# A hybrid attention layer on one core: streaming the first branch's value weights, and moving the forget gate and four modulation weights

## The chip, the cores and the metric

The kernel runs on one core of a Trainium2 chip. The metric is device time in microseconds (us). The engines are TensorE (matmuls; PE in the profile, with its weight loads as PEld), VectorE (DVE), ScalarE (ACT), GpSimd (POOL) and SyncE (SP, which here issues the loads). "Product" below means one matmul with 512 columns.

## The reference

One decoder layer for 512 tokens of width 1024, in float32. A modulation vector comes from a conditioning vector `c`. Two causal attention branches of 8 heads each run on the same modulated input:

```
mod = c @ w_ada + b_ada                        # six vectors: shift, scale, gate, twice
u = x * (1 + sc1) + sh1
q_a, k_a, v_a, f_a, q_b, k_b, v_b, g_a, g_b = split(u @ w_in)
# branch 0 (FoX): softmax(q k^T / 8 + cum_t - cum_s) v, cum = cumsum(log sigmoid(f_a + b_forget))
# branch 1 (stick-breaking): A[t,s] = beta[t,s] * prod_{s<j<t} (1 - beta[t,j]),  A v
merged = sigmoid(g_a) * (y_fox @ w_fox_proj) + sigmoid(g_b) * (y_sb @ w_sb_proj)
x = LN(alpha * x + (1 + gt1) * (merged @ w_o))
...                                            # gated MLP with a causal depthwise conv, second LN
```

## The kernel before

Every weight product is made of three matmuls: each operand is split into a high part (rounded to the matmul's format, `hi_of`, an ACT copy, line 75) and a low part (`lo_of`, a DVE subtraction, line 78), and high x high, high x low and low x high are summed. The modulated input stands as `uh[k]`, `ul[k]`, eight tiles of 128 channels by 512 tokens.

**Weights.** `items` is a list of weight blocks in the order of use, 128x1024 each. `weights(i)` lets SP load up to four items ahead into four raw buffers (tag `raw`), and lets ACT and DVE split up to two items ahead, by the item's own function: `split_proc` makes a high and a low 128x1024 tile, each from three rotating buffers (`wh`, `wl`). Items of the modulation matrix (`ada_proc`) lie among them. The first eight of the 24 in this part are accumulated on DVE (line 581), the others are summed on DVE with one instruction into a column (`mod_col`, lines 169 and 174).

**Filling products.** `stream` is a list of generators that issue products (`proj`, the values, `bproj`). The loop over the 16 heads (`heads`, first 8 of branch 1, then 8 of branch 0) works with three steps a head: `stage_a` (scores, line 473 and 474; then sigmoids and a scan on DVE, or softmax), `stage_b` (transposes, line 529), `stage_c` (weighted sum over the values, line 547). Between them `fill(n)` draws n products from `stream`, and `fill_to(mark)` draws until a mark. A mark is reached before the step that needs it: `v1` before the first `stage_c`, the pair's `k` before its `stage_a`. `lim` bounds how far the stream may be drawn; until n is 6 it is the mark `v0`, in front of branch 0's values.

The order on SP is that of the program. The order on the other engines comes from a planner that goes by its own cost model and takes the program's order as priority. PSUM has eight banks, which all steps share.

**Values.** For branch 1 (stick-breaking), `v_proc` splits the four value weights into sixteen 512-wide tiles (`wvh`, `wvl`) that stay, and `vproj` makes one block of 128 tokens after the other, 24 products each in one bank (lines 430 to 432). After each block `v_diff` copies the bank to SBUF (`vf`, line 392), moves it down by one row with transfers on POOL's queue (`dv`, lines 396 and 397), subtracts (line 399) and splits the difference (`v_evac`). For branch 0, `vgroup` already holds four banks open, one for each block, and streams the weights (lines 446 to 448); its `v_evac` calls follow all products.

**Forget gate.** `forget(after)` computes the log of the sigmoid on ACT (lines 323 to 325), its cumulated sum on DVE (line 327) and a split (`chi`), and `decay_rows` sends rows of it with POOL's queue (lines 341 and 342) to the operands of branch 0's scores. It is called at the start of n = 6.

**Order of the stream.** Pair 1 of q and k, branch 1's values, pair 2, pair 3 and two gates, branch 0's values with a modulation weight behind each group, pair 4, a gate, pairs 5, 6, 7 with one modulation weight behind each projection, then gates and projections of the outputs.

Of the kernel before, what the change touches and what calls it, by code (L numbers as in the profile page):

```python
# [9 lines left out]
F32R = mybir.dt.float32r  # L10
# [6 lines left out]
P = 128  # L17
T = 512
D = 1024
KT = D // P  # L20
NB = T // P
# [24 lines left out]
def layer_kernel(ctx: ExitStack, tc: tile.TileContext, out, xT, x, cT, crow, wa0, wa1, bcol, bgt, w1, wct, wv, bf,  # L46
# [3 lines left out]
    V, S, G, PE = nc.vector, nc.scalar, nc.gpsimd, nc.tensor  # L50
# [14 lines left out]
    def bank():  # L65
        return pp.tile([P, 512], F32, name=nm("ps"), tag="ps")
# [7 lines left out]
    def hi_of(o, i, scale=1.0):  # L74
        S.activation(o, i, AF.Copy, scale=scale)  # L75

    def lo_of(o, i, hi):
        return V.tensor_tensor(o, i, fl(hi), ALU.subtract)  # L78
# [32 lines left out]
    def z(dt, s, shape=(P, 512)):  # L111
        return zp.tile(list(shape), dt, name=nm(s), tag="z", bufs=NZ)
# [7 lines left out]
    items = []  # L120
    state = {"load": 0, "proc": 0}

    def add_item(src, proc, cols=1024):
        items.append([src, proc, cols, None, None])
        return len(items) - 1

    def weights(i, ahead=AHEAD):
        while state["load"] < min(len(items), i + LOADS):
            it = items[state["load"]]
            it[3] = stg.tile([P, 1024], F32, name=nm("raw"), tag="raw", bufs=LOADS)  # L130
            nc.sync.dma_start(it[3][:, 0 : it[2]], it[0])
            state["load"] += 1
            while state["proc"] <= state["load"] - LOADS:
                process()
        while state["proc"] < min(len(items), i + 1 + ahead):
            process()
        return items[i][4]
# [18 lines left out]
    uh, ul, w1s, mods = [], [], [], []  # L156
# [164 lines left out]
    def forget(after):  # L321
        with tc.issue_after(after.ins):
            S.activation(fq[0], fq[1], AF.Abs)
            S.activation(fq[0], fq[0], AF.Exp, scale=-1.0)
            S.activation(fq[0], fq[0], AF.Ln, bias=1.0)
        V.scalar_tensor_tensor(fq[1], fq[1], 0.0, fq[0], ALU.min, ALU.subtract)
        V.tensor_tensor_scan(fq[0], ones[0:NH, 0:1].broadcast_to([NH, 512]), fq[1], 0.0, ALU.mult, ALU.add)
        hi_of(chi[:, 0, :], fq[0])
        lo_of(chi[:, 1, :], fq[0], chi[:, 0, :])
        gated.append(True)  # L330
        for h in range(4):
            if idx(0, h) - 4 in scored:
                decay_rows(h)
# [56 lines left out]
    def v_diff(j, ps):  # L390
        vf, dv = z(F32, "vf"), z(F32, "dv")
        S.activation(vf, ps, AF.Copy)
        if j == 0:
            G.memset(dv[0:1, :], 0.0)
        else:
            G.dma_start(dv[0:1, :], vfs[-1][P - 1 : P, :])
        G.dma_start(dv[1:P, :], vf[0 : P - 1, :])
        vfs.append(vf)
        V.tensor_tensor(dv, vf, dv, ALU.subtract)
        for half in range(2):  # L400
            v_evac(1, j, half, dv)

    def v_evac(br, j, half, ps):
        vv = z(F32R, "vv")
        v3 = vv.rearrange("s (p q d) -> s p q d", q=4, d=64)
        p3 = ps[:, half * 256 : (half + 1) * 256].rearrange("s (p q d) -> s p q d", q=2, d=64)
        hi_of(v3[:, :, 0::3, :], p3)
        lo_of(v3[:, :, 1:3, :], p3, v3[:, :, 0::3, :])
        vt[(br, j, half)] = vv
# [2 lines left out]
        o = ((h // 2) % 2) * 256 + (h % 2) * P  # L412
        return vt[(br, j, h // 4)][:, o : o + P]

    def v_proc(r):
        t = []
        for e in range(2):
            h, l = z(F32R, "wvh"), z(F32R, "wvl")
            hi_of(h, r[:, e * 512 : (e + 1) * 512])
            lo_of(l, r[:, e * 512 : (e + 1) * 512], h)  # L420
            t.append((h, l))
        return t

    def vproj(br, j, last):
        ps = bank()
        weights(last)
        tb = slice(j * P, (j + 1) * P)
        for k in range(KT):
            h, l = items[wvi[k // 2]][4][k % 2]
            PE.matmul(ps, uh[k][:, tb], h, start=k == 0, stop=False)  # L430
            PE.matmul(ps, uh[k][:, tb], l, start=False, stop=False)
            PE.matmul(ps, ul[k][:, tb], h, start=False, stop=k == KT - 1)
            yield 3
        v_diff(j, ps)

    vbk = []

    def vgroup(q, n):
        if q == 0:
            vbk.extend(bank() for _ in range(NB))  # L440
        h, l = weights(n)
        for k in (2 * q, 2 * q + 1):
            c = slice((k % 2) * 512, (k % 2 + 1) * 512)
            for j in range(NB):
                tb = slice(j * P, (j + 1) * P)
                PE.matmul(vbk[j], uh[k][:, tb], h[:, c], start=k == 0, stop=False)
                PE.matmul(vbk[j], uh[k][:, tb], l[:, c], start=False, stop=False)
                PE.matmul(vbk[j], ul[k][:, tb], h[:, c], start=False, stop=k == KT - 1)
                yield 3
        if q == 3:  # L450
            for j in range(NB):
                for half in range(2):
                    v_evac(0, j, half, vbk[j])

    def proj(n, after):
        ps = bank()
# [148 lines left out]
    sg, ma, wps = {}, {}, {}  # L605
# [46 lines left out]
    stream, sums = [], []  # L652
# [4 lines left out]
    def add_ada(n=1):  # L657
        for _ in range(n):
            if skip[0]:
                skip[0] -= 1  # L660
            elif adas[0] < 24:
                add_item(wa1[adas[0]], ada_proc(adas[0]))
                adas[0] += 1
                if adas[0] in (4, 8):
                    stream.append((ada_split, (adas[0] // 4 - 1, len(items) - 1)))
                    sums.append([len(stream) + 1, adas[0] // 4 - 1])

    marks = {}
# [12 lines left out]
    def add_bproj(br, j, after):  # L681
        if j % 2 == 0:
            wpi[br] = add_item(wp[br, j // 2], split_proc)
        stream.append((bproj, (br, j, wpi[br], after)))

    def add_pair(p):
        br, pr = seq[p]
        for c, ev in (("q", q_evac), ("k", k_evac)):
            if (c, p) in TILES:
                add_proj((c, p), lambda ps, ev=ev: ev(br, pr, ps))  # L690
                marks[(p, c)] = len(stream)
                add_ada()

    wvi = []

    def add_gate(br, j):
        add_proj(("sb" if br == 1 else "fox", j), gate_after(br, j))
        add_ada()

    gb = list(range(NG, KT))  # L700
    for p, ng in ((1, 0), (2, 0), (3, 2), (4, 1)):
        if p == 4:
            marks["v0"] = len(stream)
            for j in range(4):
                stream.append((vgroup, (j, add_item(wv[0, j], split_proc))))
                add_ada()
        add_pair(p)
        if p == 1:
            for j in range(4):
                wvi.append(add_item(wv[1, j], v_proc))  # L710
            for j in range(NB):
                stream.append((vproj, (1, j, wvi[-1])))
            marks["v1"] = len(stream)
        for _ in range(ng):
            add_gate(1, gb.pop(0))
    add_pair(5)
    marks["y1"] = len(stream)
    bj = list(range(KT))
    for p in (6, 7):
        add_pair(p)  # L720
        for _ in range(4):
            if bj:
                j = bj.pop(0)
                add_bproj(1, j, lambda m, j=j: ma.__setitem__(j, m))

    mh, ml = [], []

# [37 lines left out]
    def fill(n):  # L765
        while n > 0:
            if cur["g"] is None:
                if cur["n"] >= lim[0]:
                    return
                f, a = stream[cur["n"]]  # L770
                cur["g"] = f(*a)
            try:
                n -= next(cur["g"])
            except StopIteration:
                cur["g"] = None
                cur["n"] += 1
# [19 lines left out]
    heads = [(br, 2 * p + e) for br, p in seq for e in range(2)]  # L796
    last = hd[heads[1]]['last']
    for n, (b, h) in enumerate(heads):
        if n == 6:
            forget(last)  # L800
        f1, f2, f3 = FILL[n // 8]
        if n + 2 < 16:
            if n == 6:
                lim[0] = marks["y1"]
            if n % 2 == 0:
                fill_to(marks[(n // 2 + 1, "k")])
            last = hd[heads[n + 1]].get("last")
            stage_a(*heads[n + 2])
        fill(f1)
        if n + 1 < 16:  # L810
            stage_b(*heads[n + 1])
        fill(f2)
        if n == 0:
            fill_to(marks["v1"])
            fill(15)
        stage_c(b, h)
        if n == 7:
            lim[0] = marks["y0"]
        if n == 15:
            lim[0] = len(stream)  # L820
        fill(f3)
# [133 lines left out]
    for n in range(2 * FT):  # L955
        if n < NSPLIT:
            h, l = items[wui[n]][4]
            ps = bks[n]
            up_mm(ps, h, l, slice(256, 512))
        else:  # L960
            ps = bank()
# [49 lines left out]
    for i in range(NB):  # L1011
        tb = slice(i * P, (i + 1) * P)
        r = x1[i]
# [96 lines left out]
```

## Time and profile before

| | |
|---|---|
| time of three runs | 776.55 us median, 775.83 to 776.66 |
| the profiled execution | 776.09 us, of which the span of instructions is 774.3 us |
| TensorE busy | 754.7 us in 3570 matmuls |
| VectorE busy | 541.6 us |
| ScalarE busy | 354.6 us |
| mean granted TensorE clock | 0.995 |

Times in the profile count from the start of the span. A busy row gives an engine's time in instructions; matmuls are pipelined, so their durations overlap (a product is recorded with some 0.39 us, and they follow each other at shorter distances). A row of waits reads: who waited <- for whom: us in total, times, longest. In a row of the timeline, the brackets at the end give the idle time in front of the instruction and what ended it.

### The profile page before, as it was taken

What the parts mean: (1) busy time and instruction counts of PE and PEld (TensorE: products, weight loads), DVE (VectorE), ACT (ScalarE), POOL (GpSimd) and SP (SyncE); (2) the same over time, 40 slices, a digit from 0 to 9 for tenths busy, and PEclk for the clock granted to TensorE, in tenths of its full rate; (3) what the DMA queues carried; (4) which work ended last, traced back from release to release, by engine and by line L of the source; (5) the groups of instructions that cost most, each with busy time, mean ns of one, the idle gap of its engine ahead of it and who ended that gap; (6) DMA issues with size and microseconds to landing.
All of it is one profiled execution on the core that took longest, in us unless ns stands there. A gap on an engine that the chain in (4) does not pass through costs nothing.

```text
span 774.3 us, 9546 instructions
## 1 busy us (share of the span) xinstructions
PE 754.7 (97%) x3570; PEld 622.2 (80%) x3570; DVE 541.6 (70%) x820; ACT 354.6 (46%) x592; POOL 146.2 (19%) x113
## 2 busy tenths in 40 slices
PE   8999989989999999999999999999999999999995
PEld 4878767868788888888889888888888888888885
DVE  6868748997778895476766887677656665534566
ACT  3568348854866555433145334444444433222300
POOL 1030100020100011353100680000000043945500
PEclk9999999999999999999999999999999999999998
DMA  8943621356331423444401614354332314332302
GB/s 330 404 151 135 218 82 55 117 180 221 110 114 51 137 84 131 139 165 154 149 1 55 218 58 160 110 190 135 110 109 84 106 55 163 115 103 84 106 29 81
DMA packets 31520, 100.72 MB, mean 130 GB/s; under 512 B 4433, under 2 KB 4945, under 8 KB 31474
## 3 DMA queue, kind: packets, MB, share of 16 engines
q1 hardware_dynamic: 30258, 98.72, 37.3%
q0 software_dynamic: 928, 1.11, 0.6%
q8 instruction: 28, 0.46, 0.2%
q10 hardware_dynamic: 288, 0.28, 0.1%
q14 instruction: 18, 0.15, 0.1%
HBM read 96.88 MB, written 2.10 MB: 128 GB/s over the span
## 4 chain that ended last, share of the span: by engine, by line
PE 80%; DVE 8%; issue 5%; ACT 4%; DMA 3%; POOL 0%; DVEq 0%; ACTq 0%; POOLq 0%
PE ps L115 15%; PE ps L116 15%; PE ps L117 15%; PE ps L1000 5%; PE ps L1002 5%; PE ps L1001 5%; PE ps L269 5%; PE ps L880 2%; PE ps L879 2%; PE ps L881 2%; ACT m L75 2%; PE ps L547 1%; DMA dv<-vf 1%; PE ps L473 1%; PE ps L474 1%
## 5 line engine op out<-in xcount | busy, mean ns | idle before, releaser
L78 DVE TENSOR_TENSOR wl<-raw,wh 128x1024 fp32r<-128x1024 f32 (+2 forms) x106 | 146.3, 1380 | 94.2 <-ACT wh L75 93.9
L75 ACT ACTIVATE wh<-raw 128x1024 fp32r<-128x1024 f32 (+2 forms) x106 | 110.1, 1040 | 103.1 <-PE ps L1002 38.4
L115 PE MATMUL ps<-u2h,wh 128*128 128x512 f32 (+1 forms) x376 | 141.4, 376 | 0.0
L117 PE MATMUL ps<-u2h,wl 128*128 128x512 f32 (+1 forms) x376 | 141.2, 376 | 0.0
L116 PE MATMUL ps<-u2l,wh 128*128 128x512 f32 (+1 forms) x376 | 141.2, 376 | 0.0
L639 POOL TENSOR_TENSOR raw<-raw,gt 128x1024 f32<-128x1024 f32 x22 | 59.5, 2718 | 190.9 <-DVE gt L602 157.7
L116 PEld LDWEIGHTS ps<-u2l,wh 128*128 128x128 f32 x376 | 70.8, 188 | 12.9
L115 PEld LDWEIGHTS ps<-u2h,wh 128*128 128x128 f32 x376 | 70.8, 188 | 12.9
L117 PEld LDWEIGHTS ps<-u2h,wl 128*128 128x128 f32 x376 | 70.8, 188 | 12.6
L115 PE MATMUL ps<-uh,wh 128*128 128x512 f32 x200 | 80.0, 400 | 0.0
L117 PE MATMUL ps<-uh,wl 128*128 128x512 f32 x200 | 78.8, 394 | 0.0
L116 PE MATMUL ps<-ul,wh 128*128 128x512 f32 x200 | 78.5, 392 | 0.0
L1001 PE MATMUL ps<-wl,hh 128*128 128x512 f32 x128 | 49.8, 389 | 0.0
L1000 PE MATMUL ps<-wh,hh 128*128 128x512 f32 x128 | 49.8, 389 | 0.0
L1002 PE MATMUL ps<-wh,hl 128*128 128x512 f32 x128 | 49.8, 389 | 0.0
L117 PEld LDWEIGHTS ps<-uh,wl 128*128 128x128 f32 x200 | 37.7, 189 | 8.1
L116 PEld LDWEIGHTS ps<-ul,wh 128*128 128x128 f32 x200 | 37.8, 189 | 6.8
L115 PEld LDWEIGHTS ps<-uh,wh 128*128 128x128 f32 x200 | 37.7, 189 | 6.8
L75 ACT ACTIVATE hh<-cv 128x512 fp32r<-128x512 f32 x22 | 13.9, 631 | 59.7 <-DVE cv L980 59.7
L979 ACT ACTIVATE cv<-cv 128x512 f32<-128x512 f32 x22 | 13.9, 632 | 55.2 <-DVE cv L974 55.2
L627 POOL TENSOR_TENSOR raw<-raw,gt 128x1024 f32<-128x1024 f32 x8 | 19.7, 2462 | 82.8 <-DMA raw<-in_wo 61.4
L973 DVE SCALAR_TENSOR_TENSOR cv<-ps,cw,cv 128x511 f32<-128x511 f32 x44 | 32.7, 742 | 2.3 <-ACT cv L972 2.3
(197 smaller groups left out, 1484.3 us busy)
## 6 DMA issues: line engine op xcount, KB each, us to landing
raw<-in_wup SPq DMA_DIRECT2D x44, 512.0 KB, 3.3
raw<-in_wa SPq DMA_DIRECT2D x32, 512.0 KB, 3.4
raw<-in_wct SPq DMA_DIRECT2D x25, 512.0 KB, 4.1
raw<-in_wdn SPq DMA_DIRECT2D x22, 512.0 KB, 3.4
wa<-in_wa SPq DMA_DIRECT2D x14, 512.0 KB, 7.8
raw<-in_wv SPq DMA_DIRECT2D x8, 512.0 KB, 3.4
raw<-in_wp SPq DMA_DIRECT2D x8, 512.0 KB, 4.2
raw<-in_wo SPq DMA_DIRECT2D x8, 512.0 KB, 3.9
```

What stands on the lines that cost most here:

```text
L75: S.activation(o, i, AF.Copy, scale=scale)
L78: return V.tensor_tensor(o, i, fl(hi), ALU.subtract)
L115: PE.matmul(ps, wh, ah, start=first, stop=False)
L116: PE.matmul(ps, wh, al, start=False, stop=False)
L117: PE.matmul(ps, wl, ah, start=False, stop=last)
L269: PE.matmul(grp[g], w, u, start=j == 0 and n == 0, stop=j == KT - 1 and n == (1 if g == 7 else 2))
L627: G.tensor_tensor(r, r, gt[0], ALU.mult)
L639: G.tensor_tensor(r, r, gt[1], ALU.mult)
L973: V.scalar_tensor_tensor(t[:, 1:], ps[:, 0:511], cw[:, n, 1:2], t[:, 1:], ALU.mult, ALU.add)
L1000: PE.matmul(ps, hh[j][:, tb], w[0], start=first, stop=False)
L1001: PE.matmul(ps, hh[j][:, tb], w[1], start=False, stop=False)
L1002: PE.matmul(ps, hl[j][:, tb], w[0], start=False, stop=last)
```

## The change

The first branch's values go through the same function as the second's: `vgroup` takes the branch, opens four banks at its first group and streams the weights through the rotating buffers. `v_proc` and `vproj` are gone. As soon as a block's last product is issued, its `v_diff` (branch 1) or `v_evac` (branch 0) is issued; in branch 1 all four blocks so come in the last twelve products. Before the first `stage_c`, 18 instead of 15 filling products are drawn.

The modulation weights behind branch 0's four groups are gone there; instead pairs 6 and 7 have two behind each projection. The number of them in all stays, and the ones in between each come four places later in the stream. `forget` is called after the first 36 products of branch 0's values instead of ahead of them; the mark `v0` stays at the same place.

```diff
-    def v_proc(r):
...
-    def vproj(br, j, last):
...
-    vbk = []
-
-    def vgroup(q, n):
+    vbk = {}
+
+    def vgroup(br, q, n):
         if q == 0:
-            vbk.extend(bank() for _ in range(NB))
+            vbk[br] = [bank() for _ in range(NB)]
+        ps = vbk[br]
         h, l = weights(n)
         for k in (2 * q, 2 * q + 1):
             c = slice((k % 2) * 512, (k % 2 + 1) * 512)
             for j in range(NB):
                 tb = slice(j * P, (j + 1) * P)
...
+                PE.matmul(ps[j], uh[k][:, tb], h[:, c], start=k == 0, stop=False)
+                PE.matmul(ps[j], uh[k][:, tb], l[:, c], start=False, stop=False)
+                PE.matmul(ps[j], ul[k][:, tb], h[:, c], start=False, stop=k == KT - 1)
+                if k == KT - 1:
+                    if br == 1:
+                        v_diff(j, ps[j])
+                    else:
+                        for half in range(2):
+                            v_evac(br, j, half, ps[j])
                 yield 3
-        if q == 3:
-            for j in range(NB):
-                for half in range(2):
-                    v_evac(0, j, half, vbk[j])
...
-                add_ada()
-
-    wvi = []
+                add_ada(1 + (p > 5))
+
+    def add_values(br, ada):
+        for j in range(4):
+            stream.append((vgroup, (br, j, add_item(wv[br, j], split_proc))))
+            add_ada(ada)
...
-    for p, ng in ((1, 0), (2, 0), (3, 2), (4, 1)):
-        if p == 4:
-            marks["v0"] = len(stream)
-            for j in range(4):
-                stream.append((vgroup, (j, add_item(wv[0, j], split_proc))))
-                add_ada()
+    for p, ng in ((1, 0), (2, 0), (3, 2)):
         add_pair(p)
         if p == 1:
-            for j in range(4):
-                wvi.append(add_item(wv[1, j], v_proc))
-            for j in range(NB):
-                stream.append((vproj, (1, j, wvi[-1])))
+            add_values(1, 0)
             marks["v1"] = len(stream)
         for _ in range(ng):
             add_gate(1, gb.pop(0))
+    marks["v0"] = len(stream)
+    add_values(0, 0)
+    add_pair(4)
+    add_gate(1, gb.pop(0))
     add_pair(5)
...
     for n, (b, h) in enumerate(heads):
-        if n == 6:
-            forget(last)
         f1, f2, f3 = FILL[n // 8]
         if n + 2 < 16:
             if n == 6:
                 lim[0] = marks["y1"]
+                fill(36)
+                forget(last)
...
         if n == 0:
             fill_to(marks["v1"])
-            fill(15)
+            fill(18)
         stage_c(b, h)
```

More of the change, by code (lines that the diff above doesn't have):

```diff
@@ L413, in v_part @@
         return vt[(br, j, h // 4)][:, o : o + P]
-    def v_proc(r):
[L416 to L422, printed above, removed]
-    def vproj(br, j, last):
[L425 to L434, printed above, removed]
-    vbk = []
-    def vgroup(q, n):
+    vbk = {}
+    def vgroup(br, q, n):
         if q == 0:
-            vbk.extend(bank() for _ in range(NB))
+            vbk[br] = [bank() for _ in range(NB)]
+        ps = vbk[br]
         h, l = weights(n)
@@ L445, in vgroup @@
                 tb = slice(j * P, (j + 1) * P)
-                PE.matmul(vbk[j], uh[k][:, tb], h[:, c], start=k == 0, stop=False)
-                PE.matmul(vbk[j], uh[k][:, tb], l[:, c], start=False, stop=False)
-                PE.matmul(vbk[j], ul[k][:, tb], h[:, c], start=False, stop=k == KT - 1)
+                PE.matmul(ps[j], uh[k][:, tb], h[:, c], start=k == 0, stop=False)
[7 more added lines that the diff above has]
+                            v_evac(br, j, half, ps[j])
                 yield 3
-        if q == 3:
-            for j in range(NB):
-                for half in range(2):
-                    v_evac(0, j, half, vbk[j])
     def proj(n, after):
@@ L721, in layer_kernel @@
         for _ in range(4):
-            if bj:
-                j = bj.pop(0)
-                add_bproj(1, j, lambda m, j=j: ma.__setitem__(j, m))
+            j = bj.pop(0)
+            add_bproj(1, j, lambda m, j=j: ma.__setitem__(j, m))
     mh, ml = [], []
```

## The prediction

> **What bounds the kernel now.** I read the page first, then the waits of TensorE, then the timeline around the longest of them.
>
> ```profile
> span 774.3 us, 9546 instructions
> PE 754.7 (97%) x3570; PEld 622.2 (80%) x3570; DVE 541.6 (70%) x820; ACT 354.6 (46%) x592; POOL 146.2 (19%) x113
> PE 80%; DVE 8%; issue 5%; ACT 4%; DMA 3%; POOL 0%; DVEq 0%; ACTq 0%; POOLq 0%
> ```
>
> TensorE is busy for 97% of the span and makes up 80% of the chain that ended last. The change leaves the number of products alone (96 for the values of each branch, before and after). So it can pay only where TensorE waits or runs at a lower clock, and it can cost only by making such places. The waits of TensorE, longest in total first (us in total, times, longest):
>
> ```profile
> PE ps L547 <- DVE vv L78: 3.2, 1, 3.2
> PE ps L446 <- DVE pl L78: 1.6, 1, 1.6
> PE ps L473 <- ACT m L75: 1.5, 3, 0.8
> PE ps L447 <- DVE wl L78: 0.5, 1, 0.5
> PE ps L430 <- ACT pt L506: 0.4, 1, 0.4
> ```
>
> L547 is the weighted sum of a head over the values (stage_c), L446 and L447 are the products of the second branch's values, L430 those of the first branch's. All but the third row lie where the diff works. Around the longest, TensorE's timeline (start, duration, line), and from the windows two stretches of 4 us and one of 28 us (busy time of PE, PEld, DVE, ACT, POOL, then the granted clock):
>
> ```profile
> 94.47 0.39 PE L432 MATMUL ps<-wvh,ul 128*128 128x512 f32 x1
> 94.69 0.39 PE L115 MATMUL ps<-uh,wh 128*128 128x512 f32 x1
> ...
> 98.77 0.56 PE L547 MATMUL ps<-ph,vv 128*128 128x512 f32 x2
> 102.56 0.39 PE L547 MATMUL ps<-ptc,vv 128*128 128x256 f32 x1 [3.23 <-DVE vv L78]
> ...
> 109.69 0.28 PE L547 MATMUL ps<-ptc,vv 128*128 128x256 f32 x1
> 100.00:104.00 4.00, 1.44 (x7) 1.22 (x8) 1.45 (x3) 1.21 (x3) 0.54 (x1) 0.99 0.03 11
> 104.00:108.00 4.00, 4.00 (x18) 3.25 (x16) 2.25 (x4) 1.78 (x3) 0.00 (x0) 0.58 0.37 91
> 140.00:168.00 28.00, 25.96 (x135) 20.90 (x134) 26.76 (x42) 22.09 (x37) 5.00 (x10) 1.00 0.41 133
> ```
>
> The last product of the values ends at T = 94.86 (94.47 + 0.39). Eighteen filling products follow, up to 98.77, so one takes (98.77 - 94.69)/18 = 0.227 us. Two blocks of the weighted sum go, the third waits 3.23 us, and the fourth comes at 109.69. In the four microseconds behind the wait the granted clock is 0.58, which costs up to 4.00 x 0.42 = 1.7 us. This place as a whole, with the 0.36 us at L430 (0.4 in its row), costs 3.23 + 1.7 + 0.36 = 5.3 us.
>
> **First part: the first branch's values.** Why the third block is late is seen in the shift of the values by one row (v_diff). It is a copy from PSUM, two transfers on POOL's queue (one for the first block), a subtraction and the split:
>
> ```profile
> 102.26 0.58 ACT L392 ACTIVATE vf<-ps 128x512 f32<-128x512 f32 x1
> 103.13 0.54 POOL L397 DMA_DIRECT2D dv<-vf  x1 [4.13 <-ACT vf L392]
> 106.42 0.68 DVE L399 TENSOR_TENSOR dv<-vf,dv 128x512 f32<-128x512 f32 x1
> 107.13 0.72 ACT L75 ACTIVATE vv<-dv 128x256 fp32r<-128x256 f32 x2 [1.89 <-DVE dv L399]
> 107.58 0.76 DVE L78 TENSOR_TENSOR vv<-dv,vv 128x256 fp32r<-128x256 f32 x2 [0.48 <-ACT vv L75]
> ACT vv L75: 15.6, 4
> DMA to landing us min/median/max: 2.4/3.4/7.2
> ```
>
> The copy of the last block starts at 102.26, 7.4 us after T, although its bank was complete at T. The row of 15.6 us says why: in ACT's queue each block's split stands ahead of the next block's copy, and ACT sat there four times until the transfer and the subtraction were over. The blocks go through one after the other, because their banks become complete some 24 products (5.5 us) apart.
>
> With four banks open, all four become complete within the last 12 products, 3 x 0.227 = 0.68 us apart, from T - 2.0 to T. I expect the planner to put the four copies (0.58 each) in front of the first split, since no split can be ready within 2 us. Then the transfers overlap and only POOL's issuing is serial: first copy done at T - 1.4, first issue 0.3 later at T - 1.1, seven issues of 0.54, the last of which starts at T - 1.1 + 6 x 0.54 = T + 2.1. After landing come subtraction, ACT's split and DVE's split of the first half, 1.6 us by the rows above (106.42 to about 108.0). With a landing time L the last block is ready at T + 3.7 + L: T + 7.1 with the median 3.4, T + 6.1 with 2.4, T + 10.9 with 7.2. TensorE has 18 products (4.1 us) and the first blocks (0.4 us) to do, so it arrives at T + 4.5. If nothing else is put in between, it waits 2.6 us (1.6 to 6.4). If the planner puts more work there, the wait is zero; in the timeline above 7 us of other work stand between the third and the fourth block, so it does so when it knows of the delay. I take the middle of 0 and 2.6, 1.3 us. A wait of that length has left the clock alone elsewhere (1.00 in the stretch 140 to 168, which holds the 1.6 us at L446), so the 1.7 us go as well. First part: -5.3 + 1.3 = -4.0 us, ends -5.3 and +2.8 (a wait of 6.4 with the low clock, 8.1 instead of 5.3).
>
> The Trainium skill ("DMA: Bandwidth & Descriptors", section on the anatomy of one DMA on the gpsimd path) gives about 2.0 us plus the bytes at 436 GB/s for such a transfer, which for 254 KB is 2.6 us as an estimate. It agrees with the 2.4 of the trace, and not with its 7.2. By it the wait without reordering is 1.8 us instead of 2.6 and the time 772.1.
>
> The weights of the values are now split as 128x1024 pieces into the three rotating buffers instead of sixteen 512-wide tiles that stay.
>
> ```profile
> L75 ACT ACTIVATE wvh<-raw 128x512 fp32r<-128x512 f32 x8 | 4.8, 619 | 0.0
> L78 DVE TENSOR_TENSOR wvl<-raw,wvh 128x512 fp32r<-128x512 f32 x8 | 5.3, 682 | 0.0
> L78 DVE TENSOR_TENSOR wl<-raw,wh 128x1024 fp32r<-128x1024 f32 x97 | 137.3, 1416 | 94.2 <-ACT wh L75 93.9
> ```
>
> DVE does four splits of about 1.2 to 1.4 us instead of eight of 0.68, no difference. The third and fourth groups' splits can start only when a buffer is given back, one group (24 products, 5.5 us) ahead. ACT and DVE need some 2.5 us for one, so I cost it at nothing, and the cover is that group; were it gone, each of the four splits would cost up to 2.5 us. Four banks of eight are held for 22 us. The scoring and the transposes of a head need three at a time, and the remaining four hold them; the value products themselves keep TensorE going meanwhile. Nothing for that too.
>
> **Second part: forget gate and modulation weights.** The later stretch to which four modulation weights go, and what the forget gate does among the second branch's values:
>
> ```profile
> 240.00:290.00 50.00, 49.45 (x266) 41.39 (x265) 44.85 (x90) 30.66 (x71) 2.40 (x1) 1.00 0.27 92
> 147.66 1.28 ACT L324 ACT_TABLE_LOAD   x1
> ...
> 154.08 1.28 ACT L505 ACT_TABLE_LOAD   x1
> 156.32 1.21 DVE L327 TENSOR_TENSOR_SCAN fq<-ones,fq 8x512 f32<-8x512 f32 x1
> L169 DVE SCALAR_TENSOR_TENSOR raw<-raw,cbc 128x1024 f32<-128x1024 f32 x16 | 19.6, 1223 | 10.6 <-DMA raw<-in_wa 10.6
> L174 DVE TENSOR_TENSOR modc<-modr,bcols 128x1 f32<-128x1 f32 x30 | 4.4, 155 | 0.2
> ```
>
> In the stretch of the second branch's values, 140 to 168 above, DVE is busy 26.76 of 28 us, and TensorE waits there for DVE's drains of banks and for a weight split (1.57 + 0.47 = 2.0 us). The forget gate sits in its middle: two of its table loads switch ACT between sigmoid and the logarithm and back, the scan takes DVE for 1.21 us. Behind the 36 products these come when the scores of the head before are through, and four modulation weights of about 1.4 us (1.223 + 0.155) leave DVE as well. I take both waits as gone: -2.0 us (ends -2.0 and 0).
>
> The forget gate moves eight transfers in POOL's queue later by about 36 x 0.227 = 8.2 us:
>
> ```profile
> 166.31 0.50 POOL L342 DMA_DIRECT2D m<-chi  x1
> 198.34 0.36 PE L474 MATMUL ps<-m,s 68*128 68x256 f32 x1 [0.36 <-issue]
> ```
>
> The last of them is issued at 166.31 and its rows are first read at 198.34. 32 us cover a shift of 8; nothing stands behind them in POOL's queue, so this costs nothing. The loads of the four weights move in the order written by hand for SP; each waits only for one of four raw buffers.
>
> Where they go, pairs 6 and 7, DVE has 50 - 44.85 = 5.2 us idle in 50, and four more weights take 4 x 1.38 = 5.5. TensorE loses under 0.6 us there now (49.45 of 50). All 5.5 on the path is one end, none the other. The weights have no reader for a long time and can go into gaps, so I take a value near the low end: +1.0 us.
>
> **Sum.** -4.0 - 2.0 + 1.0 = -5.0 us. The profiled execution took 776.09 us (span 774.3, 1.8 around it), which gives 771.1; the median of the runs lies 0.46 above it, so 771.6.
>
> **The rivals.** *All four blocks land late (slower).* The four transfers of 254 KB now run at the same time as each other and as the weight loads. If the last one takes the 7.2 us seen at worst, TensorE waits 6.4 us at the third or fourth block and the clock drops: 8.1 against 5.3, +2.8; with -2.0 and +1.0 this is 776.55 + 1.8 = 778.4, and 780.4 if the second part's waits stay too. It breaks even at L = 5.4 us and is slower by over 0.2% from 7.0. For it: one of four transfers already took 7.2. Against: the others took 2.4 to 3.4, and the planner may fill the time. The Trainium skill ("Trainium Kernel Development and Optimization", key constraints) says that transfers of all queues share the same 16 DMA engines and interleave, which is what this rival lives on.
>
> *DVE becomes the bound in the later stretch.* All 5.5 us of the moved weights on the path: -4.0 - 2.0 + 5.5 = -0.5, 776.1. For it: 90% busy DVE. Against: TensorE's filling products do not need those results.
>
> *The change does not do what it says at the first branch.* The planner counts on transfers faster than they are, and the wait and the low clock stay as they are: -2.0 + 1.0, 775.6.
>
> *Everything goes.* Neither the wait nor the moved weights cost anything: -5.3 - 2.0 = -7.3, 769.3.
>
> **How the numbers follow.** Forecast 0.56, everything goes 0.08, late landing 0.21, DVE bound 0.08, first part void 0.07. 0.2% is 1.55 us, about what a measurement of this kernel can tell from no change. Faster by more: 0.56 + 0.08 = 0.64. Within: 0.07 and half of the DVE case, 0.11. Slower: 0.21 and the other half, were the softmax of the later heads held up as well, 0.25. The range runs from 768.8 (everything goes, and half a microsecond of L473's waits too) to 778.6 (late landing at its price). The forecast's own range is 770 to 774.
>
> **What would show it.** Right: L547's wait under 2 us and no clock under 0.9 behind it; the four copies L392 within 2.5 us of each other; no wait of L446's group for pl or wl; DVE below 26 of 28 us while the second values run. Wrong: copies and splits alternating on ACT; landing above 5 us with a longer wait of L547; new waits of TensorE for m, wl or pt between 240 and 290.

## The result, and the profile after

The changed kernel takes 786.95 us (median of four runs, 786.73 to 789.07) against 776.61 us (775.83 to 777.9): ratio 1.0138, interval 1.0116 to 1.0160. It is slower by 10.3 us; forecast were 771.6 us, a range of 768.8 to 778.6, and a chance of 0.25 for slower. Its profiled execution took 786.92 us.

First the page of the changed kernel: span, busy times, and the shares of the chain that ended last.

```profile
span 785.1 us, 9527 instructions
PE 756.4 (96%) x3570; PEld 624.7 (80%) x3570; DVE 540.4 (69%) x816; ACT 352.7 (45%) x587; POOL 146.3 (19%) x113
PE 85%; DVE 5%; DMA 4%; ACT 3%; issue 2%; SPq 0%; DVEq 0%; ACTq 0%
```

The work is the same: as many matmuls, and 1.2 to 1.9 us less on DVE and ACT. The span grew by 10.8 us while TensorE is busy for 1.7 us more, so some 9 us are waits. TensorE's waits in the changed kernel (us in total, times, longest; L529 is the weighted sum, L511 the transposes, L426 a value product):

```profile
PE ps L529 <- DVE vv L78: 8.0, 3, 5.6
PE ps L511 <- ACT vf L392: 2.3, 1, 2.3
...
PE ps L426 <- DVE pl L78: 2.0, 1, 2.0
...
PE ps L511 <- DVE yf L536: 1.4, 1, 1.4
...
PE ps L529 <- ACT pt L488: 0.7, 1, 0.7
```

The one wait of 3.2 us at the weighted sum has become three with 8.0 us in all. The transposes now also wait 2.3 us for the copy `vf`, which reads a bank. ScalarE's timeline in the changed kernel shows where both come from (start, duration; in brackets the idle time ahead and what ended it):

```profile
92.38 0.60 ACT L392 ACTIVATE vf<-ps 128x512 f32<-128x512 f32 x1 [2.34 <-PE ps L428]
94.42 1.06 ACT L75 ACTIVATE wh<-raw 128x1024 fp32r<-128x1024 f32 x1 [1.44 <-PE ps L428]
100.17 0.72 ACT L75 ACTIVATE vv<-dv 128x256 fp32r<-128x256 f32 x2 [4.69 <-DVE dv L399]
100.80 0.58 ACT L392 ACTIVATE vf<-ps 128x512 f32<-128x512 f32 x1
...
107.28 0.72 ACT L75 ACTIVATE vv<-dv 128x256 fp32r<-128x256 f32 x2 [3.92 <-DVE dv L399]
107.91 0.58 ACT L392 ACTIVATE vf<-ps 128x512 f32<-128x512 f32 x1
...
113.95 0.58 ACT L392 ACTIVATE vf<-ps 128x512 f32<-128x512 f32 x1
119.93 0.72 ACT L75 ACTIVATE vv<-dv 128x256 fp32r<-128x256 f32 x2 [5.40 <-DVE dv L399]
```

Copy, split, copy, split: the split of each block still stands ahead of the next block's copy, although all four banks are complete at T = 94.39 (TensorE's last value product starts at 94.00 and lasts 0.39). ACT is idle for 4.7 us with three complete banks behind the waiting split. The chain that ended last shows one such round (start, duration, what):

```profile
108.00 0.49 ACT vf L392
108.49 0.28 issue
108.78 3.70 DMA dv<-vf
...
112.60 0.70 DVE dv L399
```

Copy, issue, landing, subtraction, split: the four copies start at 92.38, 100.80, 107.91 and 113.95, 6.0 to 8.4 us apart. Now the same chain in the kernel before, whose first and third copies stand in ScalarE's timeline as

```profile
78.44 0.60 ACT L392 ACTIVATE vf<-ps 128x512 f32<-128x512 f32 x1 [1.31 <-PE ps L432]
...
97.08 0.60 ACT L392 ACTIVATE vf<-ps 128x512 f32<-128x512 f32 x1
```

From its first copy to the start of its last split it took 107.13 - 78.44 = 28.7 us; in the changed kernel 119.93 - 92.38 = 27.6 us. The chain is as long as it was. It starts 13.9 us later, because no block is complete before all are nearly complete, and the value products that covered its first half now lie in front of it.

The first round is the longest (8.4 us), and VectorE's timeline of the changed kernel shows a part of the reason: a modulation piece (L563) stands ahead of the first subtraction and waits for its load. The block's transfer, issued at 93.29, had landed by 98.7 (5.4 us is the longest of the four), so the subtraction at 99.45 came at least 0.8 us late.

```profile
97.64 0.75 DVE L563 SCALAR_TENSOR_TENSOR ac<-raw,cTs,ac 128x512 f32<-128x512 f32 x1 [3.86 <-DMA raw<-in_wa]
98.31 1.22 DVE L78 TENSOR_TENSOR wl<-raw,wh 128x1024 fp32r<-128x1024 f32 x1
99.45 0.69 DVE L399 TENSOR_TENSOR dv<-vf,dv 128x512 f32<-128x512 f32 x1
```

The clock fell as well. Windows of the changed kernel (busy time of PE, PEld, DVE, ACT, POOL, granted clock, DMA share, GB/s):

```profile
100.00:104.00 4.00, 2.72 (x9) 2.24 (x10) 2.08 (x5) 2.27 (x4) 1.05 (x2) 0.83 0.80 252
104.00:108.00 4.00, 3.96 (x18) 2.88 (x16) 1.58 (x3) 0.72 (x3) 0.00 (x0) 0.74 0.78 290
...
120.00:124.00 4.00, 1.75 (x5) 1.36 (x5) 1.44 (x3) 1.97 (x5) 0.00 (x0) 0.50 0.00 0
124.00:128.00 4.00, 3.27 (x11) 2.68 (x12) 3.46 (x6) 3.98 (x10) 0.00 (x0) 0.50 0.00 0
128.00:132.00 4.00, 4.00 (x16) 3.21 (x16) 3.24 (x6) 1.65 (x4) 0.00 (x0) 0.76 0.00 0
```

TensorE's busy time times the missing share of the clock gives up to 0.5 + 1.0 + 0.9 + 1.6 + 1.0 = 5.0 us. With the waits around this place (8.0 + 2.3 + 1.4 + 0.7 = 12.4) it costs up to 17.4 us, where by the same count it cost 5.3 before: +12.1. The whole span grew by 10.8.

### The profile page after: what moved, and what is told of

The parts are those of the page before. It is cut to its first block, busy times and chain, and to the rows that moved or that the text cites. A ratio compares the mean times of both kernels' runs of the same rounds, so it can differ in the third digit from the quotient of the medians.

```text
span 785.1 us, 9527 instructions
## 1 busy us (share of the span) xinstructions
PE 756.4 (96%) x3570; PEld 624.7 (80%) x3570; DVE 540.4 (69%) x816; ACT 352.7 (45%) x587; POOL 146.3 (19%) x113
## 4 chain that ended last, share of the span: by engine, by line
PE 85%; DVE 5%; DMA 4%; ACT 3%; issue 2%; SPq 0%; DVEq 0%; ACTq 0%
PE ps L115 17%; PE ps L116 16%; PE ps L117 16%; PE ps L981 5%; PE ps L980 5%; PE ps L982 5%; PE ps L269 4%; PE ps L529 2%; PE ps L859 2%; PE ps L861 2%; PE ps L860 2%; DMA dv<-vf 2%; PE ps L511 1%; PE ps L426 1%; PE ps L428 1%
## 5 line engine op out<-in xcount | busy, mean ns | idle before, releaser
L78 DVE TENSOR_TENSOR wl<-raw,wh 128x1024 fp32r<-128x1024 f32 (+2 forms) x110 | 150.6, 1370 | 104.0 <-ACT wh L75 101.8
L75 ACT ACTIVATE wh<-raw 128x1024 fp32r<-128x1024 f32 (+2 forms) x110 | 114.5, 1043 | 110.9 <-PE ps L982 38.4
L75 ACT ACTIVATE hh<-cv 128x512 fp32r<-128x512 f32 x22 | 13.9, 631 | 59.6 <-DVE cv L960 59.6
L959 ACT ACTIVATE cv<-cv 128x512 f32<-128x512 f32 x22 | 13.9, 632 | 54.9 <-DVE cv L954 54.9
```

## The experiments

Theory 1: the order on ScalarE's queue. A split that needs a transfer stands ahead of copies that need nothing, so the four blocks go through one after the other. Rivals: the banks held open and the streamed weights starve the head; the transfers themselves are slow; the second part is to blame. Ratios are to the kernel before, run beside each kernel.

**One part at a time.** The first part alone (changed kernel, second part undone):

```diff
-                add_ada(1 + (p > 5))
+                add_ada()
...
-    add_values(0, 0)
+    add_values(0, 1)
...
+        if n == 6:
+            forget(last)
...
-                fill(36)
-                forget(last)
```

> The first part alone: four open banks and streamed weights for the first branch's values, 18 products behind; the forget gate and the modulation weights stay as before. Theory 1 (in ScalarE's queue each block's split stands in front of the next block's copy, so the four shifts run one after the other from the end of the products): 785 to 788 us, TensorE waits 8 us or more at the weighted sum of the first head. Rival 2 (four banks held for 22 us starve scoring and transposes): also 785 to 788. Rival 3 (the second part costs the time): 775 to 778.

Measured: 789.5 us, ratio 1.0144 (1.0098 to 1.0190), with 9.7 us of waits for `vv`; that is 1.5 us above what theory 1 had expected at most. The whole loss is in the first part.

The second part alone (kernel before, with the modulation weights and the forget gate moved):

```diff
-                add_ada()
+                add_ada(1 + (p > 5))
...
-                add_ada()
...
-        if n == 6:
-            forget(last)
...
+                fill(36)
+                forget(last)
```

> The kernel before with the second part alone: forget gate behind 36 products of the second branch's values, four modulation weights moved to pairs 6 and 7. Theory 1 and rival 2: within 2 us of before (774.5 to 778), since the waits at 168 to 174 and at 205 in the changed kernel are about as long as those at 159 to 166 before. Rival 3: 783 or more.

Measured: 772.54 us, ratio 0.9937 (0.9914 to 0.9960), 4.9 us faster by the ratio; I had expected less. TensorE's wait for `pl` in this kernel:

```profile
PE ps L446 <- DVE pl L78: 0.7, 1, 0.7
```

and the window of it in which the moved weights now lie (columns as above):

```profile
240.00:290.00 50.00, 50.00 (x268) 41.85 (x267) 42.91 (x84) 28.53 (x66) 2.40 (x1) 1.00 0.29 95
```

The wait for `pl` fell from 1.6 to 0.7, the one for `wl` is gone, and TensorE is busy for the whole 50 us in which the moved weights could have cost something. The rival that blames the second part falls.

**The order alone.** The changed kernel with the same instructions, in which all four blocks' copies and transfers are written ahead of the first subtraction and split:

```diff
+    dvs = []
...
-        V.tensor_tensor(dv, vf, dv, ALU.subtract)
-        for half in range(2):
-            v_evac(1, j, half, dv)
+        dvs.append(dv)
+        if j == NB - 1:
+            for i in range(NB):
+                V.tensor_tensor(dvs[i], vfs[i], dvs[i], ALU.subtract)
+                for half in range(2):
+                    v_evac(1, i, half, dvs[i])
```

> The changed kernel with the four blocks' copies and transfers written ahead of all subtractions and splits. Theory 1: the four transfers overlap, the last split is ready some 8 us behind the last product instead of 26, TensorE's wait at the first weighted sum falls from 8 us to under 3, and the time to 773 to 777. Rival 2: 784 or more, since the banks are held as long. Rival 4 (the transfers themselves are slow, 3.4 to 5.6 us, since they run beside the weight loads): together they take longer still, 779 to 783.

Measured: 776.08 us, ratio 0.9973 (0.9951 to 0.9996). ScalarE's timeline of this kernel:

```profile
91.61 1.96 ACT L394 ACTIVATE vf<-ps 128x512 f32<-128x512 f32 x3 [2.34 <-PE ps L433]
...
94.62 0.58 ACT L394 ACTIVATE vf<-ps 128x512 f32<-128x512 f32 x1
99.06 0.72 ACT L75 ACTIVATE vv<-dv 128x256 fp32r<-128x256 f32 x2 [3.86 <-DVE dv L404]
...
104.57 0.72 ACT L75 ACTIVATE vv<-dv 128x256 fp32r<-128x256 f32 x2 [0.21 <-DVE dv L404]
```

TensorE's waits in it for the values and for `pl`:

```profile
PE ps L534 <- DVE vv L78: 2.8, 1, 2.8
PE ps L431 <- DVE pl L78: 2.0, 1, 2.0
```

and, from the view of the tile `vf`, the time from issue to landing of its transfers:

```profile
DMA to landing us min/median/max: 5.3/5.7/6.1
```

The last copy starts 3.0 us after the first, the transfers overlap, the last split starts at 104.57 instead of 119.93, and the wait of the transposes for a bank is gone. Four banks are opened and the weights are streamed as in the changed kernel, so these two don't make the 10 us, and that rival falls. The banks go back earlier here (the last copy starts at 94.62 and not at 113.95), but holding them longer was a result of the order. Theory 1 holds. It isn't a gain on the second part alone, though (0.9973 against 0.9937): a wait of 2.8 us for `vv` stays, and the one of 2.0 us for `pl` is followed by a clock of 0.59 (window 160 to 164).

**The transfers alone.** The changed kernel with its order as it is, but the shift of the values by one row left out (the subtraction reads `vf` twice, and the zero for the first row goes too):

```diff
...
-            G.dma_start(dv[0:1, :], vfs[-1][P - 1 : P, :])
-        G.dma_start(dv[1:P, :], vf[0 : P - 1, :])
...
-        V.tensor_tensor(dv, vf, dv, ALU.subtract)
+        V.tensor_tensor(dv, vf, vf, ALU.subtract)
```

> The changed kernel without the seven transfers on GpSimd's queue: the difference is taken of the copy with itself, so the shift by a row is left out; copies, subtractions and splits stay, and so does their order. Theory 1: without a transfer in the chain the order costs little (each block about 2 us of ScalarE and VectorE), 770 to 774 us, which is also what the rest of the change is worth. Rival 2: 780 or more.

Measured: 771.26 us, ratio 0.9913 (0.9883 to 0.9942); the wait for `vv` is 1.3 us. Alternating copies and splits cost little if the split has nothing slow to wait for. It takes both, the transfer and the copy queued behind the split that waits for it.

**The order without the four banks.** The kernel before with the second part, each block's subtraction and split written behind the next block's copy and transfers:

```diff
-    vfs = []
+    vfs, dvs = [], []
...
-        V.tensor_tensor(dv, vf, dv, ALU.subtract)
-        for half in range(2):
-            v_evac(1, j, half, dv)
+        dvs.append(dv)
+        for i in ([j - 1] if j else []) + ([j] if j == NB - 1 else []):
+            V.tensor_tensor(dvs[i], vfs[i], dvs[i], ALU.subtract)
+            for half in range(2):
+                v_evac(1, i, half, dvs[i])
```

> The kernel before with the second part, and with one more edit in its own values: the subtraction and split of block j are written behind the copy and transfers of block j+1, block after block as before (24 products apart). Theory 1 (the order of copy and split in ScalarE's queue sets when the shift is done): the wait of 3.3 us at the weighted sum and the low clock behind it go, 4 to 5 us under the second part alone, so 767 to 770 us. Rival 4 (the transfers' landing times set it, whatever the order): the wait stays above 2 us and the time within 1.5 us of the second part alone.

Measured: 767.29 us, ratio 0.9892 (0.9871 to 0.9912). The wait for `vv` is 1.7 us:

```profile
PE ps L549 <- DVE vv L78: 1.7, 1, 1.7
```

Without the first part this brings about what that part was forecast to bring: 0.45%, or 3.5 us, on top of the second part alone (4.0 us were forecast).

**The same in the changed kernel**, to compare it with all copies first:

> The changed kernel with each block's subtraction and split written behind the next block's copy, four banks and 18 products as they are. ScalarE then has copy 0, copy 1, split 0, copy 2, split 1, copy 3, splits 2 and 3: two serial rounds fewer than in the changed kernel, two more than with all copies first. Theory 1: 778 to 783 us, between 787 and 776. If only the first copy's delay counts: 776.

Measured: 774.38 us, ratio 0.9960 (0.9945 to 0.9975), better than I had expected. The wait for `vv` is 2.8 us, as with all copies first. To let one block's copy past the split is enough to undo the loss. Against 0.9892 in the kernel before, the first part as a whole costs some 0.7% with the same late split, although 18 filling products stand there and not 15. Which of its pieces costs that (the blocks that become complete together, the four banks, the streamed weights) was not tried one by one.

**Cover.** Twice the filling products, `fill(36)` for `fill(18)`: in the changed kernel, and in the one with all copies first.

> The changed kernel with 36 instead of 18 filling products before the first weighted sum and nothing else: cover without the order. Theory 1 (the order in ScalarE's queue makes a serial chain of some 26 us behind the last product): 4.1 us more of cover leave most of the waits, 780 to 784 us. Rival (too little cover was the fault, the order does not matter): 769 to 773, as the copies-first kernel with 36.

> The copies-first kernel with 36 instead of 18 filling products in front of the first weighted sum, 4.1 us more of cover. There the wait was 2.8 us with the half clock behind it. Theory 1: both go, 771 to 773 us. Rival (the four overlapping transfers, 5.3 to 6.1 us each, are not what TensorE waits for): 775 to 777, as with 18.

The changed kernel stays slower than before: 783.34 us, ratio 1.0065 (1.0040 to 1.0089). Its profiled execution, from which the rows are, took 779.24 us. Its first and last copy in ScalarE's timeline:

```profile
91.74 0.60 ACT L392 ACTIVATE vf<-ps 128x512 f32<-128x512 f32 x1 [2.34 <-PE ps L428]
...
114.25 0.58 ACT L392 ACTIVATE vf<-ps 128x512 f32<-128x512 f32 x1
```

and its waits for `vv`:

```profile
PE ps L529 <- DVE vv L78: 6.5, 2, 4.0
```

Four more microseconds of cover don't reach the end of a chain of 28. With all copies first they do nearly: 769.1 us, ratio 0.9913 (0.9892 to 0.9934), the longest wait for `vv` 1.6 us. I had expected 771 to 773.

**The halves of the second part.** In the kernel before, the forget gate moved alone and the modulation weights moved alone:

> The kernel before with the forget gate alone moved behind 36 products of the second branch's values. If the forget gate's scan and table loads made the waits of 1.6 and 0.5 us there, this gives most of the second part's gain: 773 to 775 us. If the modulation weights made them: within 1 us of before.

> The kernel before with the four modulation weights alone moved to pairs 6 and 7. If VectorE's load by the weights made the waits at the second values: 773 to 775 us. If the moved weights crowd VectorE later, as one rival of the prediction had it: above before. If the forget gate alone counts: within 1 us of before.

Measured: 777.41 us, ratio 1.0018 (1.0004 to 1.0032) for the forget gate, and 774.71 us, ratio 0.9973 (0.9955 to 0.9991) for the weights. The gate alone gains nothing: TensorE's wait for `pl` grew from 1.6 to 2.8 us,

```profile
PE ps L446 <- DVE pl L78: 2.8, 1, 2.8
```

and the clock in the window behind it is 0.57:

```profile
164.00:168.00 4.00, 4.00 (x12) 3.13 (x12) 3.94 (x5) 0.14 (x1) 0.77 (x2) 0.57 0.35 121
```

Both together give more than the sum of the two (0.9937), so the gate pays only once the weights have left the place. That VectorE's load is the reason (it is busy for 3.94 of the 4 us) is a reading of this row and was not tried by itself.

**A better version.** The late split in the kernel before with the second part, as above, and 24 filling products for 15:

```diff
-            fill(15)
+            fill(24)
```

> The late-split kernel of the old values, with 24 instead of 15 filling products in front of the first weighted sum, 2.0 us more of cover. Its wait there was 1.7 us without a drop of the clock. If that wait goes and nothing comes instead: 1 to 2 us under the late-split kernel, 765 to 766.5 us. If the first head's late weighted sum delays the next step: 767 or more.

Measured: 766.26 us (765.73 to 766.69), ratio 0.9852 (0.9829 to 0.9876). TensorE no longer waits at the weighted sum, and the clock there is full, as a window of this kernel shows:

```profile
100.00:104.00 4.00, 4.00 (x24) 3.50 (x23) 3.29 (x4) 1.90 (x4) 0.00 (x0) 1.00 0.38 114
```

It beats the kernel before by 1.5% and the changed one by 2.8% (0.9852 / 1.0138 = 0.972). What the nine more products add to the late split is less sure: 0.4%, with intervals that just overlap. More cover without the late split was not tried in the kernel before.

## Why the prediction was wrong, point by point

**The step that failed** is "I expect the planner to put the four copies (0.58 each) in front of the first split, since no split can be ready within 2 us." The premise is true; the first split did not start until 100.17, 5.8 us after T. The planner did not act on it. "Copies and splits alternating on ACT" was named as the sign of the forecast being wrong, and it is what ScalarE's timeline shows. The row of 15.6 us had told this already: the planner of the kernel before, with blocks 5.5 us apart, had put each split ahead of a copy that was ready. I took the cause to be that the banks become complete one after the other, and that four banks would remove it. The cause was that the order written in `v_diff` (copy, transfers, subtraction, split, block by block) serves as priority; four banks left that as it was. The experiments show that the written order decides. Which duration the planner's cost model gives a transfer, and whether a longer one would have changed the order, was not tried.

**The first part**, forecast at -4.0 us, measures +1.44%, or +11.2 us. The ends of its term, -5.3 and +2.8, did not hold it, because both took the overlap for granted. What the formula T + 3.7 + L is worth where the transfers do overlap is seen in the kernel with all copies first. There T is 93.61, POOL's last issue starts at 95.88 (T + 2.3, forecast T + 2.1), and L is 5.3 to 6.1, so it gives T + 9.0 to 9.8. The last split ends at 106.34 (105.59 + 0.75), T + 12.7, as VectorE's timeline of that kernel shows:

```profile
98.33 0.69 DVE L404 TENSOR_TENSOR dv<-vf,dv 128x512 f32<-128x512 f32 x1 [0.23 <-DMA dv<-vf]
99.97 0.69 DVE L404 TENSOR_TENSOR dv<-vf,dv 128x512 f32<-128x512 f32 x1 [0.95 <-DMA dv<-vf]
...
104.46 1.22 DVE L78 TENSOR_TENSOR wl<-raw,wh 128x1024 fp32r<-128x1024 f32 x1
105.59 0.75 DVE L78 TENSOR_TENSOR vv<-dv,vv 128x256 fp32r<-128x256 f32 x2
```

Two terms were mis-sized: L (3.4 taken), and the work behind the landing, which I counted for one block only (1.6 us). From the first landing to 106.34 VectorE works through four subtractions, eight splits, a modulation piece and a weight's split, with 1 us idle in 8.

The wait itself stood elsewhere than I had put it. I took the first blocks as ready when TensorE arrives and let it wait for the last one. TensorE's timeline of the same kernel shows the opposite:

```profile
101.14 1.22 PE L534 MATMUL ps<-ph,vv 128*128 128x512 f32 x2 [2.77 <-DVE vv L78]
...
107.68 0.28 PE L534 MATMUL ps<-ptc,vv 128*128 128x256 f32 x1
```

It waits 2.8 us for the first block, whose transfer had landed only at about 98.3, and comes to the last block at 107.68, 1.3 us after its split, with other work in between. So even in the right order the wait is 2.8 us and not 1.3. The low clock, taken as gone with the wait, is there too (0.73 from 100 to 104). Whether a wait of this length brings it depends on more than its length, as the last section shows; the prediction had gone by a single wait of 1.6 us that had left the clock alone.

**Holding four banks** was costed at nothing, with the banks held for 22 us. The last bank was not given back then, but only when its copy ran at 113.95, and the cover named there, the value products, had ended at T. The transposes waited 2.3 us for it. This need not be a cost of its own: the first half of the third block's split was ready only at 114.81 and the last block's at 120.80 (by VectorE's rows), so TensorE could go on only then (at 120.86), whatever the bank did. With copies first this wait doesn't occur. The streamed weights' splits cost nothing, as forecast: TensorE has no wait for `wl` or `wh` among the first branch's products.

**The Trainium skill** ("DMA: Bandwidth & Descriptors", anatomy of one DMA) gave 2.6 us as an estimate for such a transfer. The 2.4 us with which the prediction compared it belong to a row of 2 KB (L396); the four transfers of 254 KB (L397) took 2.7 to 7.2 us before, 3.7 to 5.4 us in the changed kernel, and 5.3 to 6.1 us when they overlapped. The measurement decides; nothing in the sum had rested on the page.

**The second part**, forecast at -1.0 (-2.0 for the waits, +1.0 for VectorE in the later stretch), measures -4.9 us alone. The sign was right, and the size was missed on both sides: the moved weights cost TensorE nothing, and of the 2.0 us of waits 0.7 stay. In the profiled executions the gain is 2.8 us of span (774.3 to 771.5). Some of the rest may be the clock: its mean over a run has the median 0.994 in the kernel before and 0.9955 with the second part, by estimate 0.0015 x 775 = 1.2 us. Inside the changed kernel the gain is not seen: 1.0138 against 1.0144 without it, and the wait for `pl` is 2.0 us there. But the second interval is wide (1.0098 to 1.0190), so a gain of up to some 4 us could hide in it. How much is lost there, and why, stays open.

**The rivals.** "All four blocks land late" had the sign right, with the wrong mechanism and size: it let the transfers run at the same time, the last one landing after 7.2 us, and gave 778.4 to 780.4. In fact they ran one after the other, at 3.7 to 5.4. VectorE did not become the bound in the later stretch. The rival that the first part is void came nearest: the pattern did stay as it was. But it priced that at no change, where the same chain, begun 13.9 us later with the value products no longer beside it, costs 11 us. That is the case that was missing: a chain kept at its length and moved behind its own cover.

## What to carry to other kernels

When a step is batched, list for each in-order queue the sequence that it will run, in the order in which the program writes it; where an instruction that waits for a transfer stands ahead of one that is ready, the batch can run serially however many buffers it has, as it did here. Before producers are brought together at the end, ask which work covered the consumers' chain while they were spread out. The cheap remedy here was a few lines: issue the next block's copy before the last block's split.

## What the runs showed of the hardware

Transfers of the same 254 KB from SBUF to SBUF landed after 2.7 to 7.2 us in the kernel before and after 3.7 to 5.4 us in the changed one, where the blocks went one at a time, and after 5.3 to 6.1 us when four overlapped. The single rows of 2 KB on the same queue took about as long: 2.4 to 4.1, 3.4 to 5.6 and 5.3 to 6.1 us.

The granted clock does not go by the length of a wait alone. TensorE's wait of 2.1 us that ended at 101.28 in the changed kernel was followed by 0.83 and 0.74 (the windows from 100 to 108), and one of 2.8 us by 0.57 (the forget gate alone). A wait of 2.0 us was not, as the changed kernel's value product in TensorE's timeline

```profile
172.37 0.50 PE L426 MATMUL ps<-wh,uh 128*128 128x512 f32 x1 [1.96 <-DVE pl L78]
```

and the window behind it show:

```profile
172.00:176.00 4.00, 3.63 (x16) 3.02 (x17) 3.94 (x7) 1.93 (x4) 0.00 (x0) 1.00 0.13 40
```

A wait of the same 1.96 us with all copies first was followed by 0.59, and one of 3.05 us (98.02 to 101.07 in the kernel with the weights alone moved) left the clock at 1.00. The clock records of the traces tell what parts them. Between the start and the tail of the kernel the clock is either full or half, and in each trace it changes only on a grid of 3.41 us: in the changed kernel it is half from 102.63 for 3.41 us and from 116.28 for 13.65 us, full for 10.24 us between. Cut on that grid, TensorE's busy time decides. Two stretches of the kernel with the weights alone moved hold its 3.05 us, and a third one, of the kernel with all copies first, holds its 1.96 us:

```profile
96.22:99.63 3.41, 1.80 (x9) 1.20 (x7) 0.55 (x2) 0.00 (x0) 1.04 (x2) 1.00 0.30 77
99.63:103.05 3.42, 1.98 (x9) 1.69 (x10) 1.19 (x3) 1.61 (x4) 0.54 (x1) 1.00 0.10 22
156.42:159.83 3.41, 1.45 (x7) 0.69 (x5) 3.41 (x6) 3.39 (x7) 0.00 (x0) 1.00 0.48 159
```

In the first kernel the wait is parted between two stretches, which leave TensorE idle for 1.6 and 1.4 us; in the other it lies in one and leaves 1.96 us. In the thirteen traces every stretch at full clock with 1.89 us or more of idle time is followed by the half clock, and none with 1.66 us or less; 1.70 us was followed by it once and 1.76 us once not. So the border lies near half a stretch, and where a wait falls on the grid is luck.

It shows in the times: the twelve executions of the kernel with the weights alone moved run from 770.62 us, at a mean clock of 0.998, to 776.78 us, at 0.993.

The Trainium skill ("TensorE: Matmul & The Clock Gate", what is actually happening) has the clock halved after at least one idle window of about 3.4 us. The length of the window agrees with the grid of 3.41 us; but a window with 1.9 us of idle time in it was enough here.
